# A two-block transformer kernel whose scheduler orders the engines' instructions in its other mode

## Chip, cores and metric

One core of a Trainium2 chip runs the whole program as one launch. The metric is the device time of that launch in microseconds (us).

## What is computed

Two residual blocks on 512 tokens of width 1024, in fp32. The first holds a pooling layer and a latent-attention layer (MLA), the second holds dilated attention and an RWKV-7 recurrence side by side, and then a convolutional feed-forward. The part that matters here is the middle of the second block:

```python
att_in, rwkv_in, gate_in = jnp.split(proj, [ATT_IN, ATT_IN + RWKV_IN], axis=-1)
y_att = attention_mixer(att_in) @ w_att_out[l]
y_rwkv = rwkv7_mixer(rwkv_in, ...) @ w_rwkv_out[l]
g_att, g_rwkv = jnp.split(jax.nn.sigmoid(gate_in + b_gate[l]), N_BRANCHES, axis=-1)
x = x + gt1 * ((g_att * y_att + g_rwkv * y_rwkv) @ w_o[l])
# inside rwkv7_mixer, a scan over the 512 positions, 16 heads of 64:
sa = jnp.einsum('bhvk,bhk->bhv', state, aa_t)
state = state * w_t[:, :, None, :] + sa[..., None] * bb_t[:, :, None, :] + v_t[..., None] * k_t[:, :, None, :]
```

## The kernel before

Every large product keeps its left factor feature-major: 128x128 weight tiles against 128x512 activations, and each fp32 product is three TensorE matmuls on split operands (high by high, low by high, high by low; `mm3`, lines 193 to 195). One output tile of a 1024-wide product is 8 x 3 = 24 such matmuls in one of the two PSUM banks `mm`. Its weight arrives by DMA (`wraw`), is split by ScalarE into `whi` (line 173) and by VectorE into `wlo` (line 174), both at high priority.

The RWKV recurrence (`rwkv`) is done in chunks of 64 positions, for four batches of two feature tiles (four heads each). A batch has four parts, one after the other:

- `features` (from line 937), once per tile: decay, keys and gram matrices, a chain that goes PE (L948, L949), ScalarE, VectorE (scan), ScalarE, GpSimd, VectorE, PE (L1030) and VectorE (L1033), and ends in the transposes L1046 and L1052.
- `inverse` (from line 1061): GpSimd gathers 32x32 blocks, VectorE transposes them (L1076), solves 31 pairs of small steps (L1088, L1090), and PE (L1117, L1127) and ScalarE join the halves.
- `chain` (from line 1134): 8 steps over the chunks, each L1168 (PE), L1171 (VectorE), L1173 (PE), L1175 (ScalarE), L1180, L1157 and L1184 (PE), L1196 (VectorE). A step's accumulator is a PSUM bank `ch`.
- `outputs` (from line 1205): a group norm, PE transposes (L1236), two VectorE operations (L1238, L1239) and a write to the DRAM tile `yr_scr`.

Behind the four batches in the program text, `rwkv` calls `filler()`, which is `rest` in `program`: for four pairs of heads the attention's projections (`att_proj`, 36 output tiles of 24 matmuls) and heads (`att_heads`, lines 1326 to 1377, with one PSUM buffer `tr`), then the loads of `yr` from `yr_scr` and their splits, 8 tiles of `gates`, `att_combine` (L1415 to L1466), 8 more tiles of `gates`, and `merge`, whose products on `yr` (the first readers of all four batches) begin with two tiles of 24 matmuls.

Nothing in the text says how the two are mixed. `rwkv` and `rest` are independent until `yr`, and the order in which each engine issues them is made when the `TileContext` closes: a scheduler keeps the instructions whose inputs, in its own model of the engines, are there, and issues by priority, earlier text first. Each engine then runs its list strictly in that order, and so does each DMA queue; the large products are what the scheduler puts on PE where the recurrence, in its model, isn't ready.

## Time and profile before

| | us |
|---|---|
| three runs | 1985.28, 1985.50, 1989.89 (median 1985.5) |
| the profiled execution | 1986.21 |
| its span | 1984.4 |
| PE busy | 1913.7 (96%) |
| VectorE busy | 1270.7 (64%) |
| ScalarE busy | 888.7 (45%) |
| mean granted clock of PE | 0.993 |

The span runs from the first to the last instruction that the profiler saw; the execution is 1.8 us longer. Busy time of PE counts a matmul to its modelled end, so overlapping matmuls count once. A share is an average over stages of very different kind: the first 300 us are the pooling layer, then comes MLA until about 740 us, the RWKV projections, the recurrence mixed with attention and gates until 1481 us, and then `merge`, the output projection and the feed-forward.

### The profile page before, as it was taken

To read this page: it belongs to the slowest core of one execution; us is meant where nothing else is said; L and a number is where in the kernel's file an instruction comes from. 1 tells how busy PE (TensorE), PEld (TensorE's weight loads), DVE (VectorE), ACT (ScalarE), POOL (GpSimd) and SP (SyncE) were. 2 spreads that over 40 slices of the span, in tenths; PEclk is the share of its full clock that TensorE was granted. 3 is DMA by queue.
4 is the path that set the end of the run, shared out by engine and by line. 5 is a ranking of instruction groups with operands and counts; after the bars stand their busy time and mean duration, and the time that the engine had idled before them with its cause. 6 is when DMAs were issued, how large, how long until landed. Compare 5 with 4: busy or idle time off the path is not lost. (4 is left out here: it accounts for less than half of the span.)

```text
span 1984.4 us, 28608 instructions
## 1 busy us (share of the span) xinstructions
PE 1913.7 (96%) x10895; PEld 1558.5 (79%) x10907; DVE 1270.7 (64%) x2307; ACT 888.7 (45%) x1607; POOL 92.5 (5%) x207
## 2 busy tenths in 40 slices
PE   9999999999999999999999999989999899999998
PEld 7888887787888888777776777767767798888886
DVE  6746776868866668685575575575466566535654
ACT  5322233326655555534445555555642344423432
POOL 0000000000000000110020020020000000000002
PEclk9999999999999999999999999999999999999999
DMA  5332365675322223643542433433554603233222
GB/s 173 97 96 96 96 204 188 209 230 182 123 85 75 83 93 125 205 117 97 166 140 102 168 110 107 155 107 117 179 173 156 196 22 98 88 101 106 96 84 87
DMA packets 98377, 254.57 MB, mean 128 GB/s; under 512 B 11200, under 2 KB 15808, under 8 KB 98240
## 3 DMA queue, kind: packets, MB, share of 16 engines
q1 hardware_dynamic: 96640, 250.46, 39.3%
q8 instruction: 86, 1.41, 0.3%
q10 hardware_dynamic: 1376, 1.50, 0.2%
q0 software_dynamic: 224, 0.79, 0.1%
q14 instruction: 51, 0.42, 0.1%
HBM read 212.59 MB, written 37.75 MB: 126 GB/s over the span
## 5 line engine op out<-in xcount | busy, mean ns | idle before, releaser
L173 ACT ACTIVATE whi<-wraw 128x1024 fp32r<-128x1024 f32 (+4 forms) x293 | 289.7, 989 | 568.0 <-PE mm L194 351.9
L174 DVE TENSOR_TENSOR wlo<-wraw,whi 128x1024 fp32r<-128x1024 f32 (+4 forms) x293 | 332.0, 1134 | 198.3 <-ACT whi L173 194.2
L193 PE MATMUL mm<-hh,whi 128*128 128x512 f32 x936 | 373.1, 399 | 3.3 <-DVE cv L1554 2.4
L194 PE MATMUL mm<-hl,whi 128*128 128x512 f32 x936 | 375.6, 401 | 0.0
L195 PE MATMUL mm<-hh,wlo 128*128 128x512 f32 x936 | 372.2, 398 | 0.0
L193 PEld LDWEIGHTS mm<-hh,whi 128*128 128x128 f32 x936 | 176.8, 189 | 41.6 <-issue 4.4
L194 PEld LDWEIGHTS mm<-hl,whi 128*128 128x128 f32 x936 | 177.0, 189 | 37.8 <-issue 1.5
L195 PEld LDWEIGHTS mm<-hh,wlo 128*128 128x128 f32 x936 | 176.9, 189 | 36.0 <-issue 2.2
L194 PE MATMUL mm<-xgl,whi 128*128 128x512 f32 x416 | 163.5, 393 | 0.3 <-DVE xgl L386 0.3
L195 PE MATMUL mm<-xgh,wlo 128*128 128x512 f32 x416 | 162.1, 390 | 0.0
L193 PE MATMUL mm<-xgh,whi 128*128 128x512 f32 x416 | 161.8, 390 | 0.2 <-ACT xgh L385 0.2
L194 PE MATMUL mm<-yl,whi 128*128 128x512 f32 (+1 forms) x256 | 98.3, 384 | 0.0
L193 PE MATMUL mm<-yh,whi 128*128 128x512 f32 (+1 forms) x256 | 98.2, 383 | 0.0
L195 PE MATMUL mm<-yh,wlo 128*128 128x512 f32 (+1 forms) x256 | 98.1, 383 | 0.0
L194 PEld LDWEIGHTS mm<-xgl,whi 128*128 128x128 f32 x416 | 78.1, 188 | 17.3 <-issue 0.7
L195 PEld LDWEIGHTS mm<-xgh,wlo 128*128 128x128 f32 x416 | 78.1, 188 | 17.1 <-issue 0.7
L193 PEld LDWEIGHTS mm<-xgh,whi 128*128 128x128 f32 x416 | 78.1, 188 | 16.7 <-ACT xgh L385 0.6
L783 DVE SCALAR_TENSOR_TENSOR adaw<-adaw,cb 128x1024 f32<-128x1024 f32 x48 | 58.6, 1221 | 34.5 <-DMA adaw<-in_w_ada 33.0
L194 PE MATMUL mm<-fal,whi 128*128 128x512 f32 (+1 forms) x176 | 67.4, 383 | 0.0
L195 PE MATMUL mm<-fah,wlo 128*128 128x512 f32 (+1 forms) x176 | 67.3, 382 | 0.0
L193 PE MATMUL mm<-fah,whi 128*128 128x512 f32 (+1 forms) x176 | 67.3, 382 | 0.0
L720 ACT ACTIVATE p<-sc,nm 128x128 f32<-128x128 f32 (+1 forms) x64 | 33.7, 527 | 55.4 <-DVE nm L717 44.6
(450 smaller groups left out, 3690.5 us busy)
## 6 DMA issues: line engine op xcount, KB each, us to landing
adaw<-in_w_ada SPq DMA_DIRECT2D x48, 512.0 KB, 3.8
wraw<-in_w_up SPq DMA_DIRECT2D x41, 512.0 KB, 3.5
wraw<-in_w_at SPq DMA_DIRECT2D x36, 512.0 KB, 3.6
wraw<-in_w_pin SPq DMA_DIRECT2D x30, 512.0 KB, 3.6
wraw<-in_w_rw SPq DMA_DIRECT2D x27, 512.0 KB, 4.1
wraw<-in_w_min SPq DMA_DIRECT2D x22, 512.0 KB, 4.0
a_scr<-aqkv SPq DMA_DIRECT2D x36, 256.0 KB, 2.1
aq<-a_scr SPq DMA_DIRECT2D x36, 256.0 KB, 3.8
```

The costliest lines, as they stand in the source:

```text
L173: a = nc.scalar.activation(hi, raw, AF.Copy)
L174: b = eng.tensor_tensor(lo, raw, f(hi), ALU.subtract)
L193: nc.tensor.matmul(out, wh, ah, start=first, stop=False)
L194: nc.tensor.matmul(out, wh, al, start=False, stop=False)
L195: nc.tensor.matmul(out, wl, ah, start=False, stop=last)
L720: nc.scalar.activation(p[:, :nk], sc[:, :nk], AF.Exp, bias=nm, scale=scale, accum_out=sm)
L783: nc.vector.scalar_tensor_tensor(w, w, 1.0, K.cb, ALU.mult, ALU.mult, accum_out=K.ada[:, i:i + 1])
```

## The change

One argument. With it the scheduler asks another, more detailed model of the engines when an instruction's inputs are there; the program's text, its instructions, tiles and pools stay as they are.

```diff
--- before.py
+++ after.py
@@ -1887,7 +1887,7 @@
         arrays["in_" + k] = v
         aps[k] = nc.dram_tensor("in_" + k, v.shape, mybir.dt.from_np(v.dtype), kind="ExternalInput").ap()
     aps["out"] = nc.dram_tensor("out_0", (DT, P, S), F32, kind="ExternalOutput").ap()
-    with tile.TileContext(nc) as tc, ExitStack() as es:
+    with tile.TileContext(nc, schedule_with_timeline_sim=True) as tc, ExitStack() as es:
         program(Kern(tc, aps, es), es, aps)
     r = run_bass_kernel_spmd(nc, [arrays], core_ids=[0])
     o = r.results[0]["out_0"]
```

What it moves is seen in the order of the built program. The instructions of PE, VectorE, GpSimd and the DMA queue of SP are the same ones on both sides; on ScalarE one load of a function table stands at another line. On PE 5695 of 9566 stand at another place.

First place: PE, one step of `chain` in batch 0. The names `ch` and the arrays after the arrow belong to the recurrence, `mm` to a large product (`hh`, `hl`: the block's normed input). Before:

```order
L1168 MATMUL ch_8228<-ust0_7611,ar_7765 128x128
L1168 MATMUL ch_8228<-ust0_7611,ar_7914 128x128
L194 MATMUL mm_10407<-hl_7036,whi_10410 128x512
L195 MATMUL mm_10407<-hh_7035,wlo_10411 128x512
L193 MATMUL mm_10407<-hh_7037,whi_10410 128x512
L1173 MATMUL ch_8228<-rh0_7609,xt_8105 64x64 x4
L194 MATMUL mm_10407<-hl_7038,whi_10410 128x512
L195 MATMUL mm_10407<-hh_7037,wlo_10411 128x512
L193 MATMUL mm_10442<-hh_7023,whi_10445 128x512
```

Now, the same step, from two rows ahead of it:

```order
L194 MATMUL mm_11575<-hl_7026,whi_11578 128x512
L195 MATMUL mm_11575<-hh_7025,wlo_11579 128x512
L1168 MATMUL ch_8228<-ust0_7611,ar_7765 128x128
L1168 MATMUL ch_8228<-ust0_7611,ar_7914 128x128
L193 MATMUL mm_11575<-hh_7027,whi_11578 128x512
L194 MATMUL mm_11575<-hl_7028,whi_11578 128x512
L195 MATMUL mm_11575<-hh_7027,wlo_11579 128x512
L193 MATMUL mm_11575<-hh_7029,whi_11578 128x512
L194 MATMUL mm_11575<-hl_7030,whi_11578 128x512
```

Three matmuls of a projection stood between L1168 and L1173 before; now twenty do (with one transpose of attention). From this step's L1180 to the next one's, 9 large matmuls have become 62.

Second place: PE, one step of `chain` in batch 3, the last. Before:

```order
L1168 MATMUL ch_11150<-ust1_7615,ar_10660 128x128
L1168 MATMUL ch_11150<-ust1_7615,ar_10809 128x128
L1392 MATMUL tr_13227<-cst_84,aq_13223 128x128
L194 MATMUL mm_13543<-hl_7032,whi_13546 128x512
L195 MATMUL mm_13543<-hh_7031,wlo_13547 128x512
L193 MATMUL mm_13543<-hh_7033,whi_13546 128x512
L1173 MATMUL ch_11150<-rh1_7613,xt_11000 64x64 x4
L1326 LDWEIGHTS idb_628
L1326 MATMUL tr_13235<-amask_7331,idb_628 128x512
```

Now:

```order
L1168 MATMUL ch_11150<-ust1_7615,ar_10660 128x128
L1168 MATMUL ch_11150<-ust1_7615,ar_10809 128x128
L1173 MATMUL ch_11150<-rh1_7613,xt_11000 64x64 x4
L1180 MATMUL ch_11177<-sv_10584,bkt_10719 64x64 x2
L1180 MATMUL ch_11177<-sv_10584,bkt_10868 64x64 x2
L1157 MATMUL ch_11177<-sv_10587,g_10708 64x64
L1157 MATMUL ch_11177<-sv_10587,g_10710 64x64
L1157 MATMUL ch_11177<-sv_10587,g_10857 64x64
L1157 MATMUL ch_11177<-sv_10587,g_10859 64x64
```

Projections, gate products and attention stood between the rows; now the recurrence is alone. The last gate product now ends during the seventh of the eight steps of batch 1: after it, and until the first product on `yr`, PE has 748 instructions of two batches, of the end of batch 1 and of the last pair of heads, and no large product. From the first L948 to that point there are 1800 large matmuls and 856 small instructions; before, from the first L948 to the first product on `yr`, it was 1749 and 1604, mixed. All but a few of attention's instructions in that stretch stand ahead of the transposes L1046 of batch 2's second tile.

Third place: PE, the end of the last batch. `mm_13611` is a gate product, `mm_14135` and `mm_14170` the first two products on `yr`. Before:

```order
L1236 MATMUL sc_11315<-cst_84,yc_11294 128x128 x2
L1236 MATMUL sc_11328<-cst_84,yc_11294 128x128 x2
L1236 MATMUL sc_11315<-cst_84,yc_11302 128x128 x2
L1236 MATMUL sc_11328<-cst_84,yc_11302 128x128 x2
L195 MATMUL mm_13611<-hh_7029,wlo_13615 128x512
L193 MATMUL mm_13611<-hh_7031,whi_13614 128x512
L194 MATMUL mm_13611<-hl_7032,whi_13614 128x512
L195 MATMUL mm_13611<-hh_7031,wlo_13615 128x512
```

Now:

```order
L1236 MATMUL sc_11315<-cst_84,yc_11294 128x128 x2
L1236 MATMUL sc_11328<-cst_84,yc_11294 128x128 x2
L1236 MATMUL sc_11315<-cst_84,yc_11302 128x128 x2
L1236 MATMUL sc_11328<-cst_84,yc_11302 128x128 x2
L193 MATMUL mm_14135<-yrh_13359,whi_14138 128x512
L193 MATMUL mm_14170<-yrh_13359,whi_14173 128x512
L194 MATMUL mm_14135<-yrl_13360,whi_14138 128x512
L195 MATMUL mm_14135<-yrh_13359,wlo_14139 128x512
```

Eight gate tiles (192 matmuls) and the 24 transposes L1415 of `att_combine` stood behind the last batch and ahead of the first product on `yr`; now the products on `yr` follow at once, 4 of the L1415 stand ahead, 20 among these two products, and ten of the twelve L1460 of `att_combine` right behind them, ahead of the third product on `yr`.

## Rows read from the trace of the kernel before

**Rows 1.** The page, busy us, share of the span and number of instructions
```profile
PE 1913.7 (96%) x10895; PEld 1558.5 (79%) x10907; DVE 1270.7 (64%) x2307; ACT 888.7 (45%) x1607; POOL 92.5 (5%) x207
```

**Rows 2.** Windows of three stretches: length, busy us per engine, clock, DMA
```profile
300.00:800.00 500.00, 485.45 (x2695) 409.08 (x2695) 364.05 (x720) 251.57 (x491) 4.20 (x12) 1.00 0.44 140
800.00:1481.00 681.00, 645.20 (x4582) 497.13 (x4593) 428.80 (x895) 353.96 (x732) 70.60 (x164) 0.99 0.42 137
1481.00:1984.00 503.00, 485.15 (x2305) 406.15 (x2304) 280.51 (x389) 178.78 (x251) 14.36 (x7) 0.98 0.33 105
```

**Rows 3.** PE in time: start us, length us; 24 matmuls start from first to second row
```profile
1257.07 0.39 PE L195 MATMUL mm<-hh,wlo 128*128 128x512 f32 x1
...
1262.53 0.39 PE L195 MATMUL mm<-hh,wlo 128*128 128x512 f32 x1
```

**Rows 4.** PE in time: first L948, first and 49th matmul on `yr`
```profile
799.87 0.39 PE L948 MATMUL sc<-lwp,whi 128*128 128x512 f32 x1
...
1481.15 0.40 PE L193 MATMUL mm<-yrh,whi 128*128 128x512 f32 x1
...
1495.83 0.39 PE L193 MATMUL mm<-yrh,whi 128*128 128x512 f32 x1
```

**Rows 5.** All engines in time: one step of batch 3's `chain`, its first and last matmuls
```profile
1370.85 0.45 PE L1180 MATMUL ch<-sv,bkt 128*64 128x64 f32 x8
...
1378.54 0.60 PE L1168 MATMUL ch<-ust,ar 128*128 128x128 f32 x4
1379.18 0.43 DVE L1171 COPY rh<-ch 64x256 f32<-64x256 f32 x1 [1.78 <-PE ch L1168]
1379.78 0.68 PE L1173 MATMUL ch<-rh,xt 128*64 128x64 f32 x8
1380.49 0.38 ACT L1175 ACTIVATE sv<-ch 64x256 f32<-64x256 f32 x1 [2.25 <-PE ch L1173]
1381.28 0.45 PE L1180 MATMUL ch<-sv,bkt 128*64 128x64 f32 x8
1382.29 0.61 DVE L1196 TENSOR_TENSOR ust<-ch,up 64x128 f32<-64x128 f32 x2 [2.68 <-PE ch L1157]
1382.97 0.69 PE L1168 MATMUL ch<-ust,ar 128*128 128x128 f32 x4
...
1406.08 0.22 PE L1184 MATMUL ch<-sv,g 128*64 128x64 f32 x1
```

**Rows 6.** PE and DVE in time: batch 3, its two `features`, `inverse` and `outputs` begin
```profile
1267.84 0.40 PE L948 MATMUL sc<-lwp,whi 128*128 128x512 f32 x1
...
1299.37 0.48 PE L948 MATMUL sc<-lwp,whi 128*128 128x512 f32 x1
...
1318.40 1.27 DVE L1340 TENSOR_REDUCE mst<-tr 128x4 f32<-128x512 f32 x2
1322.97 1.95 DVE L1076 STREAM_TRANSPOSE nn<-nst 128x1024 f32<-128x1024 f32 x1 [1.50 <-POOL nst L1074]
...
1413.60 1.26 PE L1236 MATMUL sc<-cst,yc 128*128 128x128 f32 x8
```

**Rows 7.** Line L1088 (count: min/median/max ns), and PE in time after it
```profile
L1088 DVE TENSOR_TENSOR xtmp<-nn,xinv x124: 190/357/425, 869.7 to 1354.9; 128x31 f32<-128x31 f32 x8, 128x60 f32<-128x60 f32 x8, 128x87 f32<-128x87 f32 x8, 128x112 f32<-128x112 f32 x8
...
1358.74 0.69 PE L1117 MATMUL sc<-xn,g 32*32 32x32 f32 x32 [1.03 <-DVE xn L1094]
```

**Rows 8.** DMA issues 1404 to 1470 us (KB, us to landing); DVE and PE in time
```profile
yr<-yr_scr SPq DMA_DIRECT2D x8, 256.0 KB, 4.5
yr_scr<-yo SPq DMA_DIRECT2D x2, 256.0 KB, 3.0
...
1456.96 0.67 DVE L1424 TENSOR_TENSOR M<-st 8x512 f32<-8x512 f32 x1
...
1475.55 0.49 PE L1460 MATMUL sc<-w,hselr 64*128 64x512 f32 x1
```

**Rows 9.** PE in time, after `inverse` of batch 3
```profile
1363.19 0.63 PE L194 MATMUL mm<-hl,whi 128*128 128x512 f32 x1
```

## The prediction

> **What bounds the kernel now.** I read the page's busy times first: PE is busy for 1913.7 us, VectorE for 1270.7 [rows 1]. So PE sets the time, and a change that only reorders can act in two ways: it alters the 4% in which PE idles, or it opens idle time that isn't there now. The windows come second; a stretch's idle time is its length less PE's busy time [rows 2]: 14.5 us from 300 to 800 (MLA and what follows), 35.8 from 800 to 1481 (recurrence, attention, gates), 17.9 after it. At most 68 us could be won there if all of it went.
>
> The third view is the time order on PE, for what a large matmul costs: 24 of them start within 5.46 us, 0.2275 each, though each lasts 0.39 to its modelled end [rows 3]. The recurrence is of another kind. In one chain step each operation waits for the one before it on another engine [rows 5]: from L1168 at 1378.54 to the next at 1382.97 are 4.43 us, of which PE's part on that path is 0.64 + 0.71 + 1.01 (start of each of its pieces to the start of what waits for it). The reader is to see there that PE must wait in every step, and that only the large products issued in between hide it. All of them together cost the same wherever they stand; the waits are free only as long as there are products to put into them.
>
> **The change, part by part.** The order shows that seven times as many large products now fill a chain step, and that they are used up in batch 1's seventh step. Batches 2 and 3 then run alone. I sum from the first L948 on.
>
> *The dense part.* Before, 681.3 us from the first L948 to the first product on `yr` [rows 4] hold 1749 large matmuls (x 0.2275 = 397.9), 35.8 idle [rows 2], and so 247.6 for 1604 small instructions, 0.154 each. Now 51 more large ones stand behind the first L948, so it comes 51 x 0.2275 = 11.6 earlier, at 788.3. To the last gate product: 1800 x 0.2275 = 409.5, 856 x 0.154 = 132, idle 15 (between 5 and all of 35.8; low, since 62 matmuls are 14 us of cover for a 4.4 us step). That is 1345.
>
> *The end of batch 1.* A step and a half, about 8 us, and 7.5 us from the last chain matmul to `outputs` (1406.08 to 1413.60 [rows 5, 6]): 15.5.
>
> *One bare batch.* Batch 3 before took 145.8 us from its first L948 to its L1236 [rows 6], with fillers on every engine. Piece by piece without them:
> - two `features`: the first took 31.5, the second 23.6 [rows 6]. I take the second less 2.8 of attention's work, such as the 1.27 us reduction: 20.8 each, 41.5.
> - `inverse`, from L1076 to the first L1180 (1322.97 to 1370.85 [rows 5, 6]): 47.9. Its 62 small steps at 0.357 are 22 us [rows 7], on VectorE, where nothing shortens them. From L1117 at 1358.74 [rows 7] to L1180 took 12.1, with products between; I take 9, and some 6 less for VectorE's and GpSimd's fillers: 39, no lower than 31.
> - `chain`: the step above already runs at its latency, so 7 x 4.43 + 1.4 = 32.4; it took 35.2 [rows 5].
> - `outputs`: 7.5 as above.
>
> The sum is 120.5, between 105 (every piece at its lower bound) and 145.8 (no piece shrinks). Batch 2 gets 14 on top, as the last blocks of attention stand among its `features`: none if they fit its waits, 16 if both tiles take the 31.5 of the slower one. So 134.5 and 120.5.
>
> *The end of the last batch.* Before, eight gate tiles, 192 x 0.2275 = 43.7 us, hid the way of `yr` through DRAM and `att_combine`. Now nothing does. From the last L1236 to the third product on `yr`: the normed output about 3.4, its write 3.0, the read 4.5 [rows 8], the split about 1.3, 12 in all; the L1415 transposes with their copies about 12 more; from `M` to the first L1460 took 18.6 with other work between [rows 8], I take 13; the L1460 themselves about 14. That is 51, I take 50, between 40 and 60. After the third product the program is the one before: 1984.4 - 1495.83 = 488.6 [rows 2, 4].
>
> *MLA.* Its heads are spaced more evenly; its idle time bounds the gain at 14.5 [rows 2]. I take -3, and let it cost 10 at worst, a part of what the next stretch idles.
>
> *PE's clock in the bare part.* After `inverse`, where PE had waited on VectorE, a large matmul lasted 0.63 [rows 9] against 0.39 in a dense run [rows 3]: at the lower clock level, 1.6 times as long. If the bare part ran at that level throughout, a step's PE part of 2.36 us would grow by 0.6 x 2.36 = 1.4; 16 steps make 23, and PE's share of the other pieces about 10: 33. If it never fell, 0. I take 25, near the upper end, as PE will be mostly idle for 250 us, and the one wait that is there now was enough. The Trainium skill, "TensorE: Matmul & The Clock Gate", section "Part 1: The HAM clock gate", says that the lower level is the default and activity releases it, and that the level is exactly half; by it a step's PE part would double, which makes 38 in the chains and some 17 elsewhere, and the sum 30 us more. The trace's ratio of 1.6 for a matmul's length is lower than that because the length isn't all clocked work; I keep the row.
>
> *Sum.* 1345 + 15.5 + 134.5 + 120.5 + 50 + 488.6 + 25 - 3 = 2176 us of span. The profiled execution was 1.8 us longer than its span, and 0.7 above the median of three runs: **2178 us**, 9.7% slower.
>
> **The rivals.**
>
> *The bare batches don't shrink.* Both take 145.8. For it speaks that a chain step [rows 5] stands at its latency already, so what the fillers cost may be little, and that in-order queues on VectorE and ScalarE may keep late pieces of attention. Against it the 7.9 us by which the two `features` differ [rows 6], which only fillers explain. The time would be 36.6 us more, and with the clock's term doubled on `features` some 15 on top: about 2229.
>
> *The clock stays up and pieces are shorter.* The recurrence's own matmuls keep PE at the higher level: -25; each bare batch is 8 shorter: about 2137. The rows on the clock speak against it.
>
> *Not slower.* The mechanism: batch 3's `features` and `inverse` slide under batch 2's chain, as both are independent and mostly VectorE and GpSimd. It saves at most 41.5 + 39 = 80.5 of batch 3, and with all idle of the mixed stretch and of MLA gone (5 + 17.5 more) the time falls to about 2075. It would decide from 192 us of saving on, that is, when both bare batches together cost 63; the two chains alone take 65 [rows 5], the two `inverse` 62 small steps each on one engine, 44 [rows 7]. By the trace's durations that is reached only if one batch hides the whole of the other, and the order on PE has them one after the other.
>
> *The change doesn't do what it says.* The order is what each engine will run, so nothing short of other instructions could undo it; they are the same.
>
> **How the numbers follow.** The forecast gets 0.60, the batches that don't shrink 0.22, the fast clock 0.16, not slower 0.02. The forecast's own bounds (each batch by 8, the end by 10, the clock by -25 or +8, MLA by 10) make about 2130 to 2225. The range reaches to both other cases, with 2137 and 2229 inside and a margin of 20 to 25 for their own bounds: 2110 to 2250. Less than 0.3%, 6 us, couldn't be told from no change; no case ends there, so it gets 0.01, faster 0.01, slower 0.98.
>
> **What the profile after will show.** Right: a first L948 near 788; large products without gaps until about 1345, two hundred us earlier than the recurrence ends; then some 250 us in which PE's digits on the page are low, PEclk is below full, and each chain step has six pieces and no large product, 4.4 us apart at the full level and about 5.8 at the lower; the last L1236 near 1640, and the third product on `yr` about 50 us behind it; the rest as long as before. PE's busy time stays near 1914 or rises with the clock, and its share falls to about 88%. Single terms are wrong if a bare batch takes under 105 or over 146 us, if steps stay at 4.4 with the clock low, or if MLA's stretch differs by more than 15. The forecast as a whole is wrong if large products stand between the chain steps of batches 2 and 3, or if batch 3's `inverse` runs during batch 2's chain.

## The result, and the profile after

Six runs of the changed kernel have a median of 2173.88 us (2169.85 to 2180.87), six of the kernel before 1987.12. The ratio is 1.0935, with a 95% interval of 1.0916 to 1.0955: slower by 9.4%. The profiled execution took 2172.86 us, its span 2170.8. The prediction was 2178 us and 2176.

The page's busy times and its 40 slices (54.3 us each; a digit is a tenth of the slice, PEclk the granted clock):

```profile
PE 1946.7 (90%) x10907; PEld 1600.7 (74%) x10907; DVE 1270.6 (59%) x2307; ACT 890.8 (41%) x1607; POOL 92.4 (4%) x207
...
PE   9999998989999999999999998635265989999998
...
PEclk9999999999999999999999999757576999999999
```

VectorE's busy time is that of [rows 1], 1270.6 against 1270.7, and PE's has grown by 33 us: the work is the same and some of it was clocked lower. The new thing is a hole of six slices in PE's line, and PEclk falls in the same place and, in this view, nowhere else. The windows put numbers to it (length, busy us of PE, PEld, DVE, ACT, POOL, then clock, DMA share and GB/s):

```profile
300.00:801.00 501.00, 482.56 (x2671) 411.25 (x2670) 360.23 (x717) 248.18 (x487) 4.29 (x12) 0.98 0.44 137
801.00:1333.00 532.00, 529.33 (x3286) 423.23 (x3285) 261.44 (x494) 247.06 (x490) 38.21 (x83) 1.00 0.46 148
1333.00:1616.00 283.00, 140.98 (x1333) 113.17 (x1332) 152.51 (x376) 100.88 (x228) 31.70 (x81) 0.66 0.15 51
1616.00:1671.00 55.00, 25.19 (x86) 15.46 (x84) 34.13 (x51) 18.53 (x26) 0.00 (x0) 0.62 0.29 94
1671.00:2171.00 500.00, 475.29 (x2252) 397.58 (x2251) 270.45 (x377) 174.25 (x245) 14.90 (x7) 0.98 0.32 101
```

The second row is the part in which the recurrence still has fillers: PE idles 2.7 us in 532, where before it idled 35.8 in 681 [rows 2]. The third and fourth rows are the part without them: 142 of 283 us idle, then 30 of 55. The dense part got better and the rest paid for it. Of the 186.4 us between the two spans 153.4 are idle time of PE and 33.0 its busy time, by the pages.

The marks between which the time is counted, in the time order on PE:

```profile
801.31 0.39 PE L948 MATMUL sc<-lwp,whi 128*128 128x512 f32 x1
...
1332.67 0.39 PE L195 MATMUL mm<-hh,wlo 128*128 128x512 f32 x1
...
1348.41 1.97 PE L1236 MATMUL sc<-cst,yc 128*128 128x128 f32 x8 [0.66 <-DVE yc L1226]
...
1486.91 1.97 PE L1236 MATMUL sc<-cst,yc 128*128 128x128 f32 x8 [5.41 <-DVE yc L1226]
1489.29 0.80 PE L948 MATMUL sc<-lwp,whi 128*128 128x512 f32 x1 [0.42 <-DVE yo L1238]
...
1513.53 0.79 PE L948 MATMUL sc<-lwp,whi 128*128 128x512 f32 x1
...
1568.06 1.07 PE L1117 MATMUL sc<-xn,g 32*32 32x32 f32 x32 [25.72 <-DVE xn L1094]
...
1577.24 0.70 PE L1180 MATMUL ch<-sv,bkt 128*64 128x64 f32 x8 [0.47 <-ACT sv L1175]
...
1609.51 0.68 PE L1184 MATMUL ch<-sv,g 128*64 128x64 f32 x8 [0.47 <-ACT sv L1175]
...
1615.61 1.97 PE L1236 MATMUL sc<-cst,yc 128*128 128x128 f32 x8 [5.41 <-DVE yc L1226]
1622.55 1.22 PE L193 MATMUL mm<-yrh,whi 128*128 128x512 f32 x2 [4.97 <-ACT yrh L187]
...
1636.73 0.60 PE L1415 MATMUL tr<-cst,mst 128*8 128x128 f32 x4 [0.23 <-ACT st L1421]
...
1658.67 1.39 PE L1460 MATMUL sc<-w,hselr 64*128 64x512 f32 x2 [15.38 <-DVE w L1453]
...
1671.23 0.79 PE L193 MATMUL mm<-yrh,whi 128*128 128x512 f32 x1
```

The row at 1332.67 is the last gate product. The wait of 25.72 us ahead of L1117 is VectorE's inverse [rows 7], with nothing on PE to hide it. At the end, the first product on `yr` waits only 4.97 us; what PE waits for longest there is attention's combine, 15.38 us ahead of L1460.

| stretch | predicted us | measured us | off by |
|---|---|---|---|
| start to the first L948, with MLA's -3 | 785.3 | 801.3 | +16.0 |
| first L948 to the last gate product's end (1332.9) | 556.7 | 531.6 | -25.1 |
| end of batch 1 | 15.5 | 15.5 | 0.0 |
| batches 2 and 3, and the end to the third product on `yr`, with the clock's 25 | 330.0 | 322.8 | -7.2 |
| the rest | 488.6 | 499.6 | +11.0 |
| span | 2176.1 | 2170.8 | -5.3 |

So the total is nearer than its terms: the bare part, which is the mechanism, came within 7.2 us, and three misses of 11 to 25 us in the other stretches nearly cancelled. That cancelling is luck, and inside the bare part terms cancel too (see the points below).

One step of the chain at the lower level and one at the full one, both in batch 2 of the changed kernel:

```profile
1455.84 1.22 PE L1168 MATMUL ch<-ust,ar 128*128 128x128 f32 x4
1457.58 1.11 PE L1173 MATMUL ch<-rh,xt 128*64 128x64 f32 x8 [0.52 <-DVE rh L1171]
1459.16 0.70 PE L1180 MATMUL ch<-sv,bkt 128*64 128x64 f32 x8 [0.47 <-ACT sv L1175]
...
1461.49 1.22 PE L1168 MATMUL ch<-ust,ar 128*128 128x128 f32 x4
...
1474.40 0.71 PE L1168 MATMUL ch<-ust,ar 128*128 128x128 f32 x4 [0.21 <-DVE ust L1196]
1475.63 0.68 PE L1173 MATMUL ch<-rh,xt 128*64 128x64 f32 x8 [0.52 <-DVE rh L1171]
1476.78 0.45 PE L1180 MATMUL ch<-sv,bkt 128*64 128x64 f32 x8 [0.47 <-ACT sv L1175]
...
1478.45 0.71 PE L1168 MATMUL ch<-ust,ar 128*128 128x128 f32 x4 [0.29 <-DVE ust L1196]
```

From L1168 to L1168 that is 5.65 us and 4.05. The six steps of each chain between its first and last L1168 took 28.26 us in batch 2 and 27.58 in batch 3.

### The profile page after: what moved, and what is told of

Its sections match the earlier page's. It is cut to its first block, busy times and chain, and to the rows that moved or that the text cites. A ratio compares the mean times of both kernels' runs of the same rounds, so it can differ in the third digit from the quotient of the medians.

```text
span 2170.8 us, 28646 instructions
## 1 busy us (share of the span) xinstructions
PE 1946.7 (90%) x10907; PEld 1600.7 (74%) x10907; DVE 1270.6 (59%) x2307; ACT 890.8 (41%) x1607; POOL 92.4 (4%) x207
## 4 chain that ended last, share of the span: by engine, by line
PE 74%; DMA 9%; DVE 7%; issue 6%; ACT 4%; POOL 1%; SPq 0%; DVEq 0%; ACTq 0%; POOLq 0%
PE mm L193 19%; PE mm L194 19%; PE mm L195 19%; DMA adaw<-in_w_ada 7%; PE ch L694 2%; PE sc L710 1%; PE ch L1173 1%; PE sc L1030 1%; DVE adaw L783 1%; PE sc L712 1%; PE tr L1330 1%; PE tr L687 1%; PE ch L1157 1%; PE ch L1168 1%; PE ch L1184 1%
## 5 line engine op out<-in xcount | busy, mean ns | idle before, releaser
L173 ACT ACTIVATE whi<-wraw 128x1024 fp32r<-128x1024 f32 (+3 forms) x293 | 289.2, 989 | 570.5 <-PE mm L194 372.8
L174 DVE TENSOR_TENSOR wlo<-wraw,whi 128x1024 fp32r<-128x1024 f32 (+3 forms) x293 | 332.0, 1135 | 290.0 <-ACT whi L173 276.0
L193 PE MATMUL mm<-hh,whi 128*128 128x512 f32 x936 | 367.8, 393 | 3.3 <-DVE cv L1554 2.4
L194 PE MATMUL mm<-hl,whi 128*128 128x512 f32 x936 | 368.3, 393 | 0.0
L193 PEld LDWEIGHTS mm<-yh,whi 128*128 128x128 f32 x256 | 48.1, 188 | 11.8 <-issue 1.7
```

Of the source, the lines that this page charges most:

```text
L173: a = nc.scalar.activation(hi, raw, AF.Copy)
L174: b = eng.tensor_tensor(lo, raw, f(hi), ALU.subtract)
L193: nc.tensor.matmul(out, wh, ah, start=first, stop=False)
L194: nc.tensor.matmul(out, wh, al, start=False, stop=False)
```

## The experiments

Theory A is the prediction's: the loss comes from fillers that run dry, so that two batches and the end stand bare. Theory B: the new mode's order is dear in itself, wherever the fillers stand. "Holds" are order-only dependences between PE instructions (`behind`, line 143), with no semaphore. Ratios are to the kernel before, run on the same chip; the changed kernel's is 1.0935.

### The same drain in the mode of before

In the mode of before, batch 2 (drain_old) or batch 3 (drain3_old, where 4 becomes 6) may begin only behind the last gate product:

```diff
+        K.mark['f', i] = nc.tensor.matmul(ps, ww[:, :P], lwp, start=True, stop=False)
...
+        self.lastmm = nc.tensor.matmul(out, wl, ah, start=False, stop=last)
...
+        if n == 15:
+            K.behind(K.mark['f', 4], K.lastmm)
```

> The mode of before, with one hold: batch 2's first L948 only behind the last gate product, so that batches 2 and 3 run bare as they do in the new mode. Theory A: 561 us dense (two batches mixed, all fillers), two bare batches of 129 each, an end of 56, against 696 now: 2145 to 2185 us. Theory B: the bare batches are dear only in the new mode's order; here at most 2080.

> The mode of before, with one hold: batch 3's first L948 only behind the last gate product, so that one batch runs bare instead of two. If what a bare batch costs is its wall (129) less the PE work in it (about 45), 84 us each, and the uncovered end about 35 to 40, less some idle of the mixed stretch: 1987 + 84 + 38 - 10 = 2100, between 2080 and 2115 us. If the loss is a step that comes with the first exposed piece (the end, the attention's tail) and not by the batch: near drain_old, 2150 or more.

Measured: drain_old 2179.33 us, 1.0944 (1.0919 to 1.0969); drain3_old 2095.27 us, 1.0536 (1.0503 to 1.0569). Of drain_old, the last filler, batch 3's first L948 (here L949) and L1236 (L1237), and the third product on `yr`; then two windows, of the bare batches and of the end:

```profile
1374.15 0.39 PE L196 MATMUL mm<-hh,wlo 128*128 128x512 f32 x1
...
1501.58 0.80 PE L949 MATMUL sc<-lwp,whi 128*128 128x512 f32 x1
...
1626.65 2.15 PE L1237 MATMUL sc<-cst,yc 128*128 128x128 f32 x8 [5.42 <-DVE yc L1227]
...
1684.16 0.80 PE L194 MATMUL mm<-yrh,whi 128*128 128x512 f32 x1 [0.41 <-DVE mt L1500]
```

```profile
1370.00:1627.00 257.00, 111.59 (x1103) 88.90 (x1101) 137.74 (x346) 77.11 (x160) 30.25 (x78) 0.64 0.09 29
1627.00:1680.00 53.00, 24.57 (x84) 15.07 (x82) 31.95 (x46) 18.44 (x26) 0.00 (x0) 0.63 0.29 94
```

Batch 3 takes 1626.65 - 1501.58 = 125.1 us there, against 126.3 in the changed kernel, and the end 57.5 against 55.6. So the bare batch and the bare end cost the same in either mode, and draining the fillers in the old mode reproduces the whole loss. The two spans also give the price of each: drain3_old's, 2090.9, lies 106.5 over the kernel before (one bare batch and the end), drain_old's, 2176.4, 85.5 above that (one more bare batch). By the medians, each against the kernel before on its own chip, it is 106.8 and 81.8. A batch's wall less the PE work in it, 84 us, was expected. Theory B isn't needed for a loss of this size, and for bare batches it is wrong; what it says of an order with fillers comes below, with the holds.

### What the end waits for

gend_new keeps gate tiles 8 to 15 for the end:

```diff
+                if self.late and k == 0:
+                    self.behind(m, self.mark['o', 7])
...
+        K.late = n >= 8
```

> The new mode, with one hold: gate tiles 8 to 15 (192 large matmuls, 43.7 us) only behind the last transposes L1236. Theory A: the 55.6 us from the last L1236 to the third product on yr take those 43.7 us in, and the dense stretch gets shorter by them: 2125 to 2140 us. If that end is bound by the DMA of yr and by attention's combine on VectorE and ScalarE beside it all the same (rival), nothing much is won: 2160 to 2175.

Measured: 2160.99 us, 1.0852 (1.0826 to 1.0878). It won a third of what was expected and the rival's range holds it. Of its end, PE's last L1236 (here L1241), the first of the ten L1460 that stand together (here L1467), and the third product on `yr`:

```profile
1576.91 1.97 PE L1241 MATMUL sc<-cst,yc 128*128 128x128 f32 x8 [5.42 <-DVE yc L1231]
...
1648.68 1.39 PE L1467 MATMUL sc<-w,hselr 64*128 64x512 f32 x2 [11.39 <-DVE w L1460]
...
1661.25 0.79 PE L195 MATMUL mm<-yrh,whi 128*128 128x512 f32 x1
```

The end is 84.3 us instead of 55.6: 43.7 us of gates went in and it grew by 28.7. They hide the way of `yr`, of which only 6.9 us showed, but the transposes of the combine stand between them in PE's order, one group in every 22 matmuls, and the wait for `w` still comes at the end. The combine's operands had been ready since attention ended (the changed kernel's last L1368 stands at 1404.66), and its pages stand behind those of `yr` in the program's text. That the text's order is what puts it so late was an inference, and it was tried: split_new moves attention and the combine's first stage (up to `w`) in the text ahead of batch 3, split2_new puts that stage between batch 3's `inverse` and `chain`:

```diff
+        if b == 3:
+            K.early()
         os_ = [features(2 * b, dd, svs), features(2 * b + 1, dd, svs)]
...
+            K.comb = att_combine(K, o_scr)
...
-            am = att_combine(K, o_scr)
+            am = att_combine2(K, o_scr, *K.comb)
```

> The new mode, with attention and the first stage of att_combine (up to its weights w) moved in the program's text ahead of batch 3, so that its pages come before those of batch 3; the products L1460 stay behind. Theory: what the end waits for is the combine and not yr (6.9 us), since its pages stand behind yr's in the text; now its 15.4 us of wait and 7 of transposes lie beside batch 3: the third product on yr comes about 32 us behind the last L1236 instead of 55.6, 2145 to 2158 us. Rival (yr's way through DRAM is what the end waits for): 2168 to 2178.

> The new mode, with the first stage of att_combine in the text between the inverse and the chain of batch 3 (in the last try it stood ahead of batch 3's features, which took 24 us longer, as much as the end won). If the combine's operations only have to stay out of the features' way on the in-order engines: batch 3 at 129 to 137 us, the third product on yr 32 us behind the last L1236, 2150 to 2160 us. If they cost the recurrence the same wherever they stand among it: 2166 to 2178.

Measured: split_new 2171.32 us, 1.0919 (1.0884 to 1.0953), not told apart from the changed kernel; split2_new 2166.57 us, 1.0872 (1.0823 to 1.0921). Of split_new, batch 3 with its first ScalarE operation, and the third product on `yr`:

```profile
1490.41 0.80 PE L948 MATMUL sc<-lwp,whi 128*128 128x512 f32 x1 [0.41 <-DVE yo L1238]
...
1507.19 0.66 ACT L951 ACTIVATE sg<-sc,hw 128x512 f32<-128x512 f32 x1
...
1537.84 0.80 PE L948 MATMUL sc<-lwp,whi 128*128 128x512 f32 x1
...
1640.76 1.97 PE L1236 MATMUL sc<-cst,yc 128*128 128x128 f32 x8 [5.42 <-DVE yc L1226]
...
1672.49 0.80 PE L193 MATMUL mm<-yrh,whi 128*128 128x512 f32 x1
```

The end is 31.7 us, 24 less, as expected: the combine, not `yr`, was what it waited for. But batch 3's first tile takes 47.4 us instead of 24.2, and the gain is gone: the time lies in the rival's range, though not for the rival's reason. ScalarE had the combine's operations ahead of the tile's first one (L951), which started 15.6 us after its input's last matmul had ended (L949, 1491.00 and 0.63 long). In split2_new the end is 31.4 (1636.01 to 1667.44) and batch 3, from one L1236 to the next, 143.3 instead of 128.7: 24 won, 15 given back, and the time stands at the edge of the range that was named for a cost that is the same everywhere. Where a stage is latency-bound and the engines run their lists in order, another latency-bound chain wasn't free beside it, though in the changed kernel's batch 3 PE is busy for only 56.1 of 126.3 us and VectorE for 67.7.

### PE's clock

Useless matmuls into a bank that nothing reads fill the wait of the bare inverses (clk_inv 90, clk_inv2 124), in clk_all the waits of the bare features too:

```diff
+        if b >= 2:
+            ps = K.bank("ch")
+            for i in range(90):
+                K.behind(nc.tensor.matmul(ps, K.bonr, al, start=True, stop=True), K.mark['t', 2 * b + 1])
```

> The new mode, with 90 large matmuls of no use (20.5 us) put into the VectorE wait of the inverse of batches 2 and 3, where PE idles 26 to 29 us; they go to a bank of their own that nothing reads. Clock theory: after the inverse PE is then at its full level, the join (9 us) and the first two or three chain steps (5.65 us each) run as the later ones do (4.0): 5 to 8 us per batch, 10 to 16 in all, so 2158 to 2164 us. If PE's clock is not what makes the first steps long (an other-engine latency after the inverse instead): 2170 to 2180, steps unchanged.

> The same, and 40 more in each of the four bare features, behind L962 (16), L975, L988 and L1030 (8 each). Clock theory: PE's parts of the features (about 12 us each at the low level) shorten by a third to a half too, some 3 us per feature: 2145 to 2155 us. If the fillers themselves delay the features: above clk_inv.

> The new mode, with 124 instead of 90 useless matmuls in the inverse of batches 2 and 3, so that they reach to the join: with 90 PE idled 10 us more before it and only one chain step of batch 2 got shorter. Clock theory: the join and all steps now at the full level, 4.04 us a step; that takes about 4 us from the steps of each batch and 2 from each join: 2160 to 2167 us. If the useless matmuls or the order they force cost as much as the clock gives: 2170 or more.

Measured: clk_inv 2178.25 us, 1.0949 (1.0922 to 1.0977); clk_all 2177.02, 1.0941 (1.0915 to 1.0968); clk_inv2 2188.44, 1.0976 (1.0938 to 1.1014). None is faster than the changed kernel, so the gains that the clock theory named didn't come. In clk_inv2 the useless matmuls held the full level hardly longer than they ran. Its windows, first of batch 2, where the last useless matmul ended near 1441 and PE waited 3.9 us ahead of the join; then of batch 3, where they ran until 1580.4 and PE waited for nothing longer than 0.6 us in the next 4 us:

```profile
1460.00:1478.00 18.00, 14.40 (x115) 12.56 (x116) 3.87 (x11) 4.72 (x13) 0.00 (x0) 0.50 0.00 1
1481.00:1493.00 12.00, 7.09 (x89) 5.69 (x88) 4.05 (x11) 3.56 (x10) 1.24 (x3) 0.97 0.00 0
...
1553.00:1580.00 27.00, 27.00 (x119) 22.26 (x119) 24.28 (x56) 0.82 (x2) 0.00 (x0) 0.99 0.01 5
1580.00:1584.00 4.00, 2.96 (x106) 2.24 (x104) 0.43 (x1) 3.14 (x7) 0.00 (x0) 1.00 0.02 4
1585.00:1613.00 28.00, 22.58 (x203) 19.80 (x202) 5.44 (x16) 6.92 (x19) 0.00 (x0) 0.50 0.02 6
```

and of the changed kernel, at its batch 2 (the inverse, then the join and the first steps, then the others):

```profile
1411.00:1438.00 27.00, 0.00 (x0) 0.00 (x0) 24.77 (x66) 0.00 (x0) 0.00 (x0) 0.52 0.13 47
1438.00:1462.00 24.00, 17.65 (x234) 15.63 (x235) 4.85 (x10) 9.28 (x23) 1.64 (x3) 0.50 0.04 13
1465.00:1483.00 18.00, 11.14 (x141) 9.13 (x139) 7.23 (x19) 6.00 (x16) 1.24 (x3) 1.00 0.00 1
```

In clk_inv2 the level came back only near 1482 in batch 2 and near 1615 in batch 3, so that the six steps took 31.3 us in both, 3.0 and 3.7 more than in the changed kernel. So the wait of 3.9 us isn't what cost the level: batch 3 lost it without one. In clk_inv, whose useless matmuls ended 11 us ahead of the join in batch 2 and 7 us in batch 3, the steps took 25.1 and 27.8: 3.2 won in the one and nothing in the other. What a chain gains or loses by the clock is thus bounded: 31.3 at the lower level nearly throughout, 24.3 for six steps at the 4.05 of the full one, 7 us per chain. In the bare features the clock decides little. In clk_all the first feature of batch 3, at a granted clock of 0.73 instead of 0.57, took 24.9 us instead of 24.2, but there two of PE's pieces stood right behind useless matmuls, so that these may have cost what the clock gave. In the second, at 0.93 instead of 0.56, the last L1046 (here L1057) came 24.5 us behind the feature's L948 (L955) instead of 25.7: 1.2 us won where 3 were expected. What the clock is worth in the rest of the inverse stays open.

### Spreading the fillers by holds

Can the new mode be mended by spreading the fillers? In p_new each third of a filler tile may be issued only behind a named matmul of the recurrence, with a quota for each place; p_old has the same holds in the mode of before.

```diff
+                if self.plan and k in (0, 3, 6):
+                    key = self.plan.pop(0)
+                    if key is not None:
+                        self.behind(m, self.mark[key])
...
+    quota = [('f0', 5), ('g0', 3), ('f1', 5), ('g1', 3), ('t1', 14)] + [('c%d' % j, 2) for j in range(1, 8)] + [('e7', 3)]
```

(f is L948, g the last L1030, t the last L1052 of a tile, c a step's L1168, e the last step's L1184.)

> The new mode, but each third of a filler tile (attention projections, gate products, the recurrence's own later projections) may be issued only behind a named matmul of the recurrence: 46 to 47 thirds per batch, 2 per chain step, 14 in the inverse, the last 8 gate tiles behind the last chain step. Theory A (the fillers run dry in batch 1, and two bare batches and the end pay for it): the 283 us with PE half idle disappear; what stays is the 13 us of MLA and the 7 us at the end of the feed-forward, so 1975 to 2005 us. Theory B (the new mode's order is dear in itself, in the recurrence's own queues or in MLA): over 2080.

> The same holds in the mode of before. Theory A: the fillers are spread as evenly as the scheduler did by itself, so 1965 to 2000 us, a little under the new mode with the same holds because MLA keeps its order. Theory B says nothing else here; what it needs is that this kernel is faster than the new mode with holds by 80 us or more.

Measured: p_new 2128.62 us, 1.0688 (1.0671 to 1.0704); p_old 2028.92 us, 1.0192 (1.0174 to 1.0210). Both miss what theory A expected: p_new wins back a quarter of the loss, and p_old is slower than the kernel before. The 100 us between the two are more than the 80 that theory B named, and p_new lies over its 2080: by what was laid down here the new mode's order has a price of its own once fillers stand among all four batches, though the bare batches show none. So the finer pair, p2c_new and p2c_old: three matmuls at a time, sized by the waits of the bare batches, and the combine's first stage ahead of the loads of `yr`.

```diff
+                if self.plan:
...
+    quota = [('a0', 6), ('s0', 4), ('r0', 3), ('g0', 4), ('a1', 6), ('s1', 4), ('r1', 3), ('g1', 4), ('t1', 48)] + [('c%d' % j, 2) for j in range(1, 8)] + [('e7', 28)]
...
+            comb = att_combine(K, o_scr)
```

(a is L962, s the last L975, r the last L988.)

> The new mode with holds again, three matmuls at a time, and sized by the waits that the bare batches of the changed kernel show: 17 times three in each of two features, 48 in the inverse, 2 in each chain step, 28 behind the last step (the first holds put 15 to 24 matmuls where PE waits 1 to 5 us); and att_combine's first stage ahead of the loads of yr, with gate tiles 8 to 15 behind the last step as cover. Theory C (what decides is that no lump of fillers is longer than the wait it stands in): a batch takes 160 to 170 us instead of 190, the end 60 to 65 instead of 88: 1985 to 2030 us. If the grain doesn't matter: 2100 to 2130.

> The holds and the earlier combine of the last kernel, in the mode of before. Under the first, coarser holds the mode of before was 100 us faster than the new one with the same holds. Theory D (with equal spread, what is left between the modes is which of two ready things the scheduler puts first on PE: the new mode lets fillers and attention go ahead of the recurrence's next piece, and PE's pauses then also cost the clock): again 70 to 110 us under the new mode's 2097, 1985 to 2025, with the granted clock of the stretch from 800 to 1600 at 0.96 or more. If the finer holds leave the scheduler no choice, the two modes come together: 2050 or more.

Measured: p2c_new 2096.81 us, 1.0527 (1.0492 to 1.0561); p2c_old 2035.28 us, 1.0209 (1.0175 to 1.0242). The finer grain won 32 us in the new mode, all of it in the batches (709 us instead of 745), less than the 98 or more of theory C; the end, from the last L1236 to the third product on `yr`, got no shorter (76.9 us, then 79.9). The modes are 61 us apart: p2c_old's time lies between the ranges of theory D and its rival, and its clock from 800 to 1600, 0.95, is under the 0.96 of theory D. Neither is settled by it. Windows from the first L948 to the last L1236, of p_new:

```profile
805.00:1550.00 745.00, 639.23 (x4450) 511.15 (x4461) 404.21 (x861) 335.31 (x704) 64.95 (x164) 0.91 0.36 116
```

of p2c_new:

```profile
806.00:1515.00 709.00, 623.54 (x4384) 495.47 (x4383) 399.42 (x858) 329.29 (x698) 65.52 (x164) 0.92 0.37 119
```

and of p2c_old, with the stretch behind it:

```profile
805.00:1416.00 611.00, 557.34 (x4004) 431.07 (x4013) 381.09 (x830) 296.40 (x619) 67.09 (x164) 0.94 0.37 119
1416.00:1525.00 109.00, 107.64 (x579) 83.09 (x582) 45.66 (x61) 57.25 (x112) 0.00 (x0) 1.00 0.54 184
```

Under the same holds the four batches take 709 us in the new mode and 611 in the old, about what they took before (799.87 to 1413.60 [rows 4, 6], 614), and the old one leaves more fillers for the stretch behind. So the holds only say when a filler may come; the rest of the order the mode still decides, and nothing else differs between these two kernels. Which of its choices makes the 98 us wasn't tried. And a wait that the holds open shows twice: PE idles 54 us in p2c_old's 611 where the kernel before idled 33 in 614, and its granted clock there is 0.94 instead of 0.99, so that the fillers take longer too. None of the twelve kernels beats the kernel before. Why its scheduler's simpler model mixes better here than the detailed one stays open: the runs show its order, not its reasons.

## Why the prediction was right, point by point

- **That the fillers run dry in batch 1 and two batches stand bare: right.** The last gate product ended at 1332.9, predicted 1345, and nothing large stands between the chain steps of batches 2 and 3. drain_old makes the loss again in the other mode, so this is shown and not only argued. That the total came within 5 us is luck; by its own steps the sum gives 2177 and not 2178.
- **One bare batch, 120.5 and 134.5 us:** from one L1236 to the next 128.7 and 138.5, with the clock's part, which the sum held apart. By pieces for batch 3 (L948 at 1489.29): `features` 47.3 (to L1076 at 1536.62) for 41.5, `inverse` 40.6 for 39, `chain` 32.3 for 32.4, `outputs` 6.1 for 7.5. The term that was too small is `features`: I took 2.8 us off the 23.6 of [rows 6] for attention's work, but bare the two took 24.2 and 23.1, so that feature already ran at about its latency; the clock accounts for little over 1 us in the one feature of clk_all where it can be read. Not counted were 2.4 us from the last L1236 to the next L948.
- **A chain step, 4.43 us "at its latency":** no, it is 4.05. Of the 0.38 between them, 0.35 lie between L1173 and L1180 (1.50 in [rows 5], 1.15 bare), where fillers stood in the row that I read. The lower level made it 5.65, near the 5.8 forecast. That the chain's term fitted is two errors that cancel.
- **The clock, 25 us of at most 33, 23 of these in the steps: too large there.** I had PE near the lower level for all 16 steps. The six steps of the rows above took 28.26 and 27.58 instead of 24.3, together 7.2 us for 12 steps, since the full level came back during each chain. What the clock cost in the other pieces no run separates. A step grew by 1.6 us at the lower level, where the row's ratio gave 1.4. The windows show 0.50 in the join and the first steps and 1.00 afterwards. The Trainium skill, "TensorE: Matmul & The Clock Gate", section "Part 1: The HAM clock gate", by which the lower level is exactly half, agrees with these two levels; a doubling of the step's whole PE part would have made it 2.36, and that the trace doesn't show.
- **The end, 50 us: 55.6, but put together wrongly.** I gave 12 us to `yr`'s way through DRAM. It shows with 6.9, since the first products on `yr` read tiles of earlier batches, and two products (14 us) run ahead of the combine. The combine, from the first L1415 behind those (1636.73) to the third product, took 34.5. gend_new shows that the same gates don't hide it where its last transposes (1631.66) come behind all of them: PE idled 17.0 us of those 84.3. "Before, eight gate tiles hid the way of `yr` and the combine" was right, but because the last L1415 (1456.82) had 18.7 us of cover between itself and the first L1460. PE then idled 3.1 us in the 82.2 from the last L1236 to the third product:

```profile
1413.60:1495.83 82.23, 79.17 (x368) 58.49 (x369) 47.86 (x63) 39.40 (x65) 0.00 (x0) 1.00 0.61 204
```

- **The dense part, 556.7 us: 531.6, the largest miss.** Of it 12 us are idle time (15 taken, 2.7 measured, under my lower end of 5) and 13 are small instructions: 531.6 - 2.7 - 409.5 = 119.4 us for 856 is 0.140 each, and not the 0.154 of the stretch before. A lone small piece among large products seems to cost more than several in a row; that was not tried.
- **MLA, -3 us with bounds of -14.5 and +10: +13.3, outside.** The first product of the RWKV projections came at 790.30 instead of 777.03, behind the same wait:

```profile
339.55 2.07 PE L332 MATMUL ch<-dg,ones 128*128 128x512 f32 x2 [5.28 <-DVE dg L329]
...
790.30 0.50 PE L193 MATMUL mm<-hh,whi 128*128 128x512 f32 x1 [0.85 <-DVE zm L882]
```

  PE's largest new wait on the way is that for the norm's `dg`. From 300 on PE idles 18.4 us where it idled 14.5 [rows 2], at a clock of 0.98 instead of 1.00, which is up to 10 us more; and before 300, in the pooling layer, it idles 6.6 us where it idled 2.1. That the heads stand more evenly told nothing of the stretch ahead of them, which the sum left out. The 51 products moved behind the first L948 did bring it 11.8 us forward against that mark (11.6 forecast).
- **The rest, taken as unchanged: +11.** PE idles 24.7 us in the 500 behind the third product; before, 18.3 in the 488.6. Its waits for the norms' `dg` and `sq` in that stretch grew from 2.4 to 5.5 us, so the mode reorders there as well; the sum followed the order only at the recurrence.
- **The rivals.** Batches that don't shrink (145.8) and a clock that stays up were both wrong: 128.7 and 138.5, and a mean clock of 0.66. The one on the other side failed as argued: batch 3's `inverse` ran behind batch 2's chain, one after the other.

## What to carry to other kernels

Where a latency-bound chain is hidden behind independent work, read in the built order how far the cover reaches; a chain that outlives it costs its wall less the PE work in it, here 82 to 86 us for a batch of 126, and once more for each stage behind it that had the same cover. Cover is a budget to be spread over the whole chain: no idle time in its first half (2.7 us of 532) was a sign of waste, not of gain. And when a scheduler's mode is changed, compare the order over the whole program: the stretches that I took as nearly unchanged moved by 11 and 13 us.

## What the runs showed of the hardware that I had not expected

The lower level lasted much longer than the wait ahead of it, and it also came without one. In the changed kernel's batch 2 PE idled 29.3 us and then ran for 24 us (1438.7 to about 1463) at the lower level; in clk_inv's it idled 10.2 and the level came back after some 13. In clk_inv2's batch 2, 28 us of large matmuls at the full level were followed by a wait of 3.9 us, and PE then ran for 36 us (1445.7 to about 1482) at the lower level, though it was busy for 14.40 of 18 us in one of these windows. In its batch 3 the join followed the large matmuls with no such wait, and the level still fell near 1584 and came back near 1615. And at the full level it stayed with PE busy for only 11.14 of 18 us. So neither the busy share of a stretch, nor the work just before it, nor the length of the wait told the level here, and in these three kernels useless work ahead of a chain bought no time. What does set the level stays open.
